# Causal attention in a hybrid decoder layer: low keys zero-padded to 128 rows, value products in one 65-column group, division left to the head norm

## Chip, cores and metric

The kernel runs on one core of one Trainium2 chip. The metric is the device time of one execution in microseconds (us), the median of several runs.

## The reference, cut to what matters

One layer of a decoder trunk over 2048 tokens of width 1024. Eight attention heads of width 64 with a forget gate, and four mLSTM heads of width 128, share one input projection; their outputs are normed per head and go through `W_out`, then an MLP (1024 to 4096 to 1024) and a gated embedding follow. The part that the change touches:

```python
def fox_attention(q, k, v, f_pre):            # q, k, v: (1, 2048, 8, 64)
    c = cumsum(log_sigmoid(f_pre))            # per head
    for each block i of 128 queries:
        s = q_i @ k.T * 64 ** -0.5 + c_query - c_key
        s = where(key <= query, s, -inf)
        o_i = softmax(s) @ v
    return o

def head_rmsnorm(h, g):                       # per token and head, over 64 values
    return h * rsqrt(mean(h * h) + 1e-6) * g
```

## The kernel before

**Precision by halves.** Every operand of a matmul is float16, split into a high and a low part, so a product is a sum of three: high by high, high by low, low by high. A projection (`z_feature`, `z_token`) is 24 accumulating matmuls: 8 blocks of 128 inputs by 3.

**Stages.** In order of time: RMSNorm and transposition of x; mLSTM head by head, to about 530 us; attention in four pairs of heads, 558 to 1347 us; `W_out`, MLP and gated embeddings, from 1347 us on.

**One pair of heads.** `fox_attn` goes through both heads of a pair, and for each through nine groups of query blocks (`ROWS`: block 15, the pairs 14 and 0 to 8 and 6, block 7), so that a group has 16 key blocks, and the last has 8. For each group:

- `fox_rows` makes scores in pieces of up to 512 keys. Line 782 multiplies 128 rows of queries (64 high, 64 low) by 128 rows of keys (the high keys twice). Line 784 adds high queries by low keys, on 64 rows: rows 0 to 63 for the first head of a pair, 64 to 127 for the second, out of one tile `KL` that both heads share. Line 787 adds the mask where the piece reaches the diagonal. VectorE adds the gate bias, stores the sum and keeps the row maximum (line 790). ScalarE takes the exponential (805), then ScalarE makes the high half of the weights (810, tile `ph`, four buffers) and GpSimd, one time in eight VectorE, the low half (812). A transposing DMA on SP's queue brings both halves into `pt` (814, three buffers).
- `fill` emits pieces of other work in step with the length of the rows, from `pair_parts`: the next pair's projections (`fox_z`) and a share of `p @ W_ple` (`ple_parts`, which uses the second half of `KL`'s allocation as scratch). For the last pair the pieces are the mLSTM half of `W_out`. Projections and these pieces share four PSUM buffers, `psz`.
- `fox_av`, three groups later (`LAG`), multiplies the transposed weights by the values. A row of the value tile `vt` is a one, 64 high values, 64 low values: 129 columns. Per key block two matmuls accumulate in `av`, one PSUM bank with one buffer: high weights by all 129 columns (827), low weights by the first 65 (828). Column 0 is then the sum of weights. For each query block VectorE takes its reciprocal (834), ScalarE scales the columns of low values (836), and VectorE scales the high ones and adds (837), into `og`.
- `fox_post`, some groups later again, takes 512 tokens of a pair: squares on GpSimd (918), their sum, the inverse root by Newton steps on VectorE, the scaling, high and low halves, a transposing DMA and a store to `mixd` (a transposing DMA into `mix` for the last pair). It has a tile `po` of its own, whose halves are used in turn (`po_half`).

**Low halves of the projections.** `fox_z` has ScalarE write the high half of queries, values and keys, and VectorE the low half right behind it (lines 731, 733, 748, 755).

**Order.** Within an engine the instructions stand in the order that a planner gives them from its own estimates of durations and of free buffers; it follows the order of the program closely, but may put a score matmul among the value products of another group. Each engine then works through its list strictly in that order, and waits on semaphores.

Of the kernel before, what the change touches and what calls it, by code (L numbers as in the profile page):

```python
# [36 lines left out]
AB = 1  # L37
# [18 lines left out]
def hybrid_layer(ctx, tc, x, p, w_in, b_fox_f, b_mlstm_i, b_mlstm_f, w_conv, g_mix,  # L56
# [42 lines left out]
    def rstd_of(v, w, name, c=1.0):  # L99
        """c / sqrt(v) for v [P, w]: a first guess from the exponent and three Newton steps."""  # L100
# [59 lines left out]
    def prep_rows(w, r0, name, pool):  # L160
        """W rows r0..r0+256 (all 1024 columns) as hi and lo fp16 with one power of two."""
# [22 lines left out]
    def norm_T(pool, yp, g, xs, nm, ss=None):  # L184
        """rmsnorm (gain left out) of the 4 token tiles xs as transposed hi/lo tiles."""
# [98 lines left out]
    class Carve:  # L284
        """small tiles cut from larger ones"""
# [17 lines left out]
    def gates(gp, gpp):  # L303
# [16 lines left out]
        # columns of gz: 8 fox f, 4 mlstm i, 4 mlstm f  # L320
# [11 lines left out]
        # log_sigmoid(x) = min(x, 0) - log1p(exp(-|x|))  # L332
# [31 lines left out]
        # global cumulative sums of the fox gates, as rows  # L364
# [17 lines left out]
        # mlstm stabiliser  # L382
# [98 lines left out]
    with phase("mq", 1) as mq, phase("mbig", 1) as mb, phase("mc", 2) as mc, \  # L481
# [6 lines left out]
        for h in range(MH):  # L488
# [43 lines left out]
            # head rmsnorm of num / max(|den|, exp(-m)), times the output gate  # L532
# [42 lines left out]
    def ple_parts(sp, t0, t1):  # L575
        """p @ W_ple for token tiles t0 to t1, emitted one at a time between query rows"""
# [48 lines left out]
    # ---- W_out: weights, and the share of the mLSTM features, kept in DRAM -  # L625
# [5 lines left out]
    def wo_prep(r, b):  # L631
        """rows of half r (0: FoX, 1: mLSTM) and columns of half b"""
# [40 lines left out]
    vts, cur, fk, fhl, fst = {}, {}, {}, {}, {}  # L673

    def second_keys():
        """keys of the second head of a pair, once the pair before is through"""
# [7 lines left out]
    def pair_parts(j, box):  # L684
        """while pair j is at work: projections of the next one, a share of p @ W_ple"""
        z = fox_z(j + 1, box)
        pl = ple_parts(fk[1][:, 1], *((0, 5), (5, 10), (10, 16))[j])
# [7 lines left out]
    def fox_z(j, box):  # L695
        """projections of head pair j, emitted piece by piece; box gets what attention needs"""
# [25 lines left out]
        K, KL = fk[0], fk[1][:, 0]  # L722
        QA, QB, KA, KB = Q[:, 0], Q[:, 1], K[:, 0], K[:, 1]
        vtile(j)
        for g in range(G):
# [5 lines left out]
            V.scalar_tensor_tensor(QA[64:128, gs], ps[0:64], QS, QA[0:64, gs],  # L731
                                   ALU.mult, ALU.subtract)
            V.scalar_tensor_tensor(QB[0:64, gs], ps[64:128], QS, QB[64:128, gs],
                                   ALU.mult, ALU.subtract)
# [8 lines left out]
        for t in range(NT):  # L743
# [4 lines left out]
            V.scalar_tensor_tensor(vt[:, t, :, 65:129], src, QS, vt[:, t, :, 1:65],  # L748
                                   ALU.mult, ALU.subtract)
        for g in range(G):  # L750
# [4 lines left out]
            V.scalar_tensor_tensor(KL[0:64, gs], ps[0:64], QS, KA[0:64, gs],  # L755
                                   ALU.mult, ALU.subtract)
            V.tensor_copy(KA[64:128, gs], KA[0:64, gs])
            second.append((KB, KL, ps, gs))
        box.append((fs, iv, vt, ((QA, KA, KL, 0), (QB, KB, KL, 64))))
# [5 lines left out]
    def fox_rows(fl, fpp, h, rows, bias, fs, qkl):  # L765
        """scores and softmax weights of the query blocks rows of head h, side by side in
        units of 8 key blocks; returns the transposed weights of each unit"""
        Qt, Kt, KL, r0 = qkl
# [5 lines left out]
        for r, i in enumerate(rows):  # L774
            qs = slice(i * P, (i + 1) * P)
            mx, kb, parts = None, 0, []
            while kb <= i:
# [6 lines left out]
                PE.matmul(ps[:, 0:n * P], lhsT=Qt[r0:r0 + 64, qs], rhs=KL[r0:r0 + 64, ks],  # L784
                          start=False, stop=not diag)
# [32 lines left out]
    def fox_av(fl, fpp, h, rows, pts, vt, ogs):  # L818
        """weighted values of the query blocks, over the sums of the weights"""
        aps = fpp.tile([P, 512], F32, tag="av", name=f"av{h}_{rows[0]}", bufs=AB)  # L820
        at = 0
        for r, i in enumerate(rows):
            ar = aps[:, 256 * r:256 * r + 129]
            for kb in range(i + 1):
                pt, o = pts[(at + kb) // 8], (at + kb) % 8
                vs = vt[:, kb, (h % 2), :]
                PE.matmul(ar, lhsT=pt[:, o, :], rhs=vs, start=kb == 0, stop=False)  # L827
                PE.matmul(ar[:, 0:65], lhsT=pt[:, 8 + o, :], rhs=vs[:, 0:65],
                          start=False, stop=kb == i)
            at += i + 1  # L830
        for r, i in enumerate(rows):
            ar = aps[:, 256 * r:256 * r + 129]
            rs = fl.tile([P, 1], F32, tag="rs", name=f"rs{h}_{i}", bufs=8)
            V.reciprocal(rs, ar[:, 0:1])
            t1 = fl.tile([P, FD], F32, tag="t1", name=f"t1{h}_{i}", bufs=2)
# [4 lines left out]
    posts, avq, loads = [], [], []  # L840
# [9 lines left out]
    def mix_load(lo, hi):  # L850
        """finished mixed features back into SBUF, a piece at a time"""
# [16 lines left out]
    def fox_attn(fl, fpp, j, z, fill):  # L868
        fs, iv, vt, qkls = z
        ogs = {}  # L870
        cur[1] = 0
        cur[0] = fl.tile([P, S], F16, tag="po", name=f"po{j}", bufs=1)
        for hh in range(2):
# [9 lines left out]
            for k, rows in enumerate(ROWS):  # L883
                pts = fox_rows(fl, fpp, h, rows, bias, fs, qkls[hh])
                for i in rows:
                    if hh == 0 and i // 4 not in ogs:
                        ogs[i // 4] = fl.tile([P, 4, 2, FD], F32, tag="og",
# [22 lines left out]
    def po_half():  # L910
        cur[1] ^= 1
        return cur[0][:, cur[1] * 1024:cur[1] * 1024 + 1024]

    def fox_post(fl, j, g, og_, iv):
        """head rmsnorm of 512 tokens of a head pair, transposed into the mixed features."""
        og = og_.rearrange("p q h d -> p (q h) d")
        sq = po_half().bitcast(F32).rearrange("p (q d) -> p q d", d=FD)
# [3 lines left out]
        V.tensor_scalar(ss, ss, iv[:, 1:2], EPS, op0=ALU.mult, op1=ALU.add)  # L921
# [223 lines left out]
```

## Time and profile before

| | |
|---|---|
| time, three runs | 2997.50, 3002.49, 3008.02 us; median 3002.49 |
| span of the profiled execution | 2998.0 us, so the median lies 4.5 us above it |
| TensorE busy over the span | 2747.0 us (92%) |
| VectorE busy | 1676.0 us (56%) |
| ScalarE busy | 1049.3 us (35%) |
| GpSimd busy | 751.9 us (25%) |
| attention, from first score to last value product | about 558 to 1347 us |

In the profile PE is TensorE, PEld its weight loads, DVE VectorE, ACT ScalarE, POOL GpSimd, and SPq the queue that issues DMAs for SyncE. L784 is line 784 of the kernel before. A matmul's duration contains its way through the array, and the next one starts before it ends: what a matmul costs in a stream is the distance from its start to the next start, the pitch. A wait is written "who <- for whom".

### The profile page before, as it was taken

What the parts mean: (1) busy time and instruction counts of PE and PEld (TensorE: products, weight loads), DVE (VectorE), ACT (ScalarE), POOL (GpSimd) and SP (SyncE); (2) the same over time, 40 slices, a digit from 0 to 9 for tenths busy, and PEclk for the clock granted to TensorE, in tenths of its full rate; (3) what the DMA queues carried; (4) which work ended last, traced back from release to release, by engine and by line L of the source; (5) the groups of instructions that cost most, each with busy time, mean ns of one, the idle gap of its engine ahead of it and who ended that gap; (6) DMA issues with size and microseconds to landing.
All of it is one profiled execution on the core that took longest, in us unless ns stands there. A gap on an engine that the chain in (4) does not pass through costs nothing. (4 is left out here: it accounts for less than half of the span.)

```text
span 2998.0 us, 43441 instructions
## 1 busy us (share of the span) xinstructions
PE 2747.0 (92%) x17141; PEld 1483.3 (49%) x17141; DVE 1676.0 (56%) x3764; ACT 1049.3 (35%) x1878; POOL 751.9 (25%) x529
## 2 busy tenths in 40 slices
PE   4998999889888787888899999999999999999996
PEld 2766767454453443443344444444444444444785
DVE  6464654666858667557754454444544544445526
ACT  6244444465655564553411111111111111114432
POOL 1001100233433343243122111111121111111454
PEclk9999999999999998999999999999999999999998
DMA  9112220486876797896700000000000000003513
GB/s 246 38 44 57 57 50 22 112 156 131 146 148 132 150 200 187 190 201 218 149 29 29 29 29 29 15 26 17 29 29 28 29 29 29 28 15 70 112 43 141
DMA packets 539869, 256.27 MB, mean 85 GB/s; under 512 B 433296, under 2 KB 511376, under 8 KB 539664
## 3 DMA queue, kind: packets, MB, share of 16 engines
q1 hardware_dynamic: 529904, 236.67, 34.8%
q10 hardware_dynamic: 9760, 16.82, 1.7%
q8 instruction: 134, 2.20, 0.3%
q14 instruction: 71, 0.58, 0.1%
HBM read 113.88 MB, written 32.60 MB: 49 GB/s over the span
## 5 line engine op out<-in xcount | busy, mean ns | idle before, releaser
L1029 PE MATMUL d<-wd_hl,hid 128*128 128x512 f16 x3072 | 677.2, 380 | 10.7 <-DVE x L1034 10.6
L1011 PE MATMUL h<-y1t,wu_hl 128*128 128x512 f16 x3072 | 673.5, 379 | 2.5 <-ACT y1y L201 2.5
L1029 PEld LDWEIGHTS <-hid 128*128 128x128 f16 x3072 | 301.1, 98 | 376.6 <-issue 16.8
L1011 PEld LDWEIGHTS <-wu_hl 128*128 128x128 f16 x3072 | 300.5, 98 | 365.2 <-ACT y1y L201 3.0
L1034 DVE SCALAR_TENSOR_TENSOR x<-d,fac,x 128x512 f32<-128x512 f32 x512 | 373.5, 747 | 132.2 <-PE d L1029 132.1
L1019 POOL TENSOR_TENSOR hid<-r,hid 128x512 f16<-128x512 f32 x128 | 174.7, 1365 | 772.3 <-ACT hid L1018 666.4
L1017 DVE SCALAR_TENSOR_TENSOR r<-h,r 128x512 f32<-128x512 f32 x128 | 88.3, 690 | 461.6 <-ACT r L1015 461.5
L1015 ACT ACTIVATE r<-h 128x512 f32<-128x512 f32 x128 | 76.0, 594 | 768.9 <-PE h L1011 768.9
L812 POOL TENSOR_TENSOR ph<-sp,ph 128x1024 f16<-128x1024 f32 x119 | 255.8, 2162 | 311.5 <-ACT ph L810 216.3
L272 PEld LDWEIGHTS <-yt 128*128 128x128 f16 x3072 | 245.0, 100 | 37.0 <-issue 15.0
L261 PE MATMUL zqk<-yt,wqk_hl 128*128 128x512 f16 x768 | 188.0, 392 | 27.0 <-DMA yt<-yy 27.0
L805 ACT ACTIVATE sp<-sp,nb,fs 128x1024 f32<-128x1024 f32 (+3 forms) x192 | 179.1, 982 | 50.4 <-DVE nb L802 34.9
L991 PE MATMUL pg<-wpg_hl,y2t 128*128 128x256 f16 x1536 | 173.3, 276 | 17.6 <-ACT emb L1110 13.6
L272 PE MATMUL zvo<-wvo_hl,yt 128*128 128x256 f16 x1536 | 174.7, 275 | 4.8 <-ACT wvo_hl L156 3.5
L782 PE MATMUL s<-K,Q 128*128 128x512 f16 (+3 forms) x320 | 117.5, 367 | 62.7 <-DVE mx L790 61.1
L991 PEld LDWEIGHTS <-y2t 128*128 128x128 f16 x1536 | 151.9, 99 | 39.1 <-issue 19.7
L810 ACT CAST ph<-sp 128x1024 f16<-128x1024 f32 x136 | 139.0, 1038 | 71.5 <-DMA pt<-ph 71.3
L827 PE MATMUL av<-vt,pt 128*128 128x129 f16 x1088 | 115.5, 229 | 49.2 <-DVE og L837 29.3
L790 DVE CUSTOM_DVE_ANT_0 sp<-s,bias,mx 128x512 f32<-128x512 f32 (+2 forms) x192 | 124.0, 646 | 17.8 <-POOL ph L812 5.1
L827 PEld LDWEIGHTS <-pt 128*128 128x128 f16 x1088 | 102.8, 102 | 53.1 <-issue 31.9
L261 PEld LDWEIGHTS <-wqk_hl 128*128 128x128 f16 x768 | 77.4, 101 | 104.0 <-ACT wqk_hl L156 24.9
L642 PEld LDWEIGHTS <-mix 128*128 128x128 f16 x768 | 74.1, 101 | 99.9 <-issue 26.8
(378 smaller groups left out, 3581.3 us busy)
## 6 DMA issues: line engine op xcount, KB each, us to landing
x<-in_x_dram SPq DMA_DIRECT2D x32, 512.0 KB, 4.6
wu_st<-in_w_up_dram SPq DMA_DIRECT2D x16, 1024.0 KB
wd_st<-in_w_down_dram SPq DMA_DIRECT2D x16, 1024.0 KB, 4.9
bias<-crow SPq DMA_DIRECT2D x16, 512.0 KB, 5.1
pled<-fox_st ACTq DMA_DIRECT2D x32, 256.0 KB, 3.0
wod<-spare ACTq DMA_DIRECT2D x32, 256.0 KB, 3.5
wos<-wod SPq DMA_DIRECT2D x32, 256.0 KB, 3.5
emb<-pled SPq DMA_DIRECT2D x64, 128.0 KB, 2.1
```

The costliest lines, as they stand in the source:

```text
L261: PE.matmul(ps, lhsT=hl[:, a, kt, m * P:(m + 1) * P], rhs=yT[g][b][:, kt, :], start=i == 0, stop=i == 3 * KT - 1)
L272: PE.matmul(ps[:, 0:n], lhsT=yT[g][b][:, kt, o:o + P], rhs=hl[:, a, kt, 0:n], start=i == 0, stop=i == 3 * KT - 1)
L790: V.tensor_tensor_reduce(out=st[u][:, o * P:(o + n) * P], in0=ps[:, 0:n * P], in1=bias[kb // 8][:, kb % 8 * P:(kb % 8 + n) * P], scale=1.0 ...
L805: A.activation(sl_, sl_, AF.Exp, bias=nb, scale=fs[:, 0:1])
L810: A.copy(ph[:, 0:1024], st[u])
L812: eng.tensor_sub(ph[:, 1024:2048], st[u], ph[:, 0:1024])
L827: PE.matmul(ar, lhsT=pt[:, o, :], rhs=vs, start=kb == 0, stop=False)
L991: PE.matmul(ps, lhsT=aT[t // 4][ya][:, kt, o:o + P], rhs=hl[:, wa, kt, :], start=i == 0, stop=i == 3 * KT - 1)
L1011: PE.matmul(ps, lhsT=wu[:, a, kt, m * P:(m + 1) * P], rhs=y1T[g][b][:, kt, :], start=i == 0, stop=i == 3 * KT - 1)
L1019: T.tensor_sub(hid[:, 1, m], r2, hid[:, 0, m])
L1029: PE.matmul(ps, lhsT=hid[:, a, m, t * P:(t + 1) * P], rhs=wd[:, b, m, hf * 512:(hf + 1) * 512], start=i == 0, stop=i == 5)
L1034: V.scalar_tensor_tensor(xs, ps, fac, xs, ALU.mult, ALU.add)
```

## The change

Four edits; comment lines, which were removed as well, are left out here.

1. The low keys of the two heads of a pair get a half tile each, `KLA` and `KLB`, whose other 64 rows are set to zero once. The matmul of line 784 then takes all 128 rows of queries and of low keys.
2. A value product is three matmuls per key block into one group of 65 columns: high weights by one and high values, high weights by low values into the same columns 1 to 64, low weights by one and high values. The 65 sums are copied as they are into `og`; the division by the sum of weights is left out, and `fox_post` norms the undivided values with epsilon times the squared sum in place of epsilon. `av` becomes one tile of one bank, with two places used in turn.
3. The low halves of queries, values and keys in `fox_z` are put off (the diff shows the values'): each is emitted two pieces later, and all that are open are emitted when `fill` or `second_keys` begins.
4. `fox_post` takes its two work tiles from the ring `ph` of the softmax weights; the tile `po` is gone. `ple_parts` gets scratch of its own.

```diff
+    def defer(fn):
+        lows.append(fn)
+        if len(lows) > 2:
+            lows.pop(0)()
+    def flush():
+        while lows:
+            lows.pop(0)()
     def second_keys():
+        flush()
...
+            T.memset(fk[1][64:128, 0], 0.0)
+            T.memset(fk[1][0:64, 1], 0.0)
-        K, KL = fk[0], fk[1][:, 0]
+        K, KLA, KLB = fk[0], fk[1][:, 0], fk[1][:, 1]
...
-            V.scalar_tensor_tensor(vt[:, t, :, 65:129], src, QS, vt[:, t, :, 1:65],
-                                   ALU.mult, ALU.subtract)
+            defer(lambda t=t, src=src: V.scalar_tensor_tensor(
+                vt[:, t, :, 65:129], src, QS, vt[:, t, :, 1:65], ALU.mult, ALU.subtract))
...
-                PE.matmul(ps[:, 0:n * P], lhsT=Qt[r0:r0 + 64, qs], rhs=KL[r0:r0 + 64, ks],
-                          start=False, stop=not diag)
+                PE.matmul(ps[:, 0:n * P], lhsT=Qt[:, qs], rhs=KL[:, ks], start=False,
+                          stop=not diag)
...
-        aps = fpp.tile([P, 512], F32, tag="av", name=f"av{h}_{rows[0]}", bufs=AB)
+        if not avt:
+            avt.append(fpp.tile([P, 2, 2, P], F32, name="av", bufs=1))
+        slot[0] ^= 1
+        aps = avt[0][:, slot[0]]
...
-                PE.matmul(ar, lhsT=pt[:, o, :], rhs=vs, start=kb == 0, stop=False)
-                PE.matmul(ar[:, 0:65], lhsT=pt[:, 8 + o, :], rhs=vs[:, 0:65],
-                          start=False, stop=kb == i)
+                PE.matmul(ar, lhsT=pt[:, o, :], rhs=vs[:, 0:65], start=kb == 0, stop=False)
+                PE.matmul(ar[:, 1:65], lhsT=pt[:, o, :], rhs=vs[:, 65:129], start=False,
+                          stop=False, skip_group_check=True)
+                PE.matmul(ar, lhsT=pt[:, 8 + o, :], rhs=vs[:, 0:65], start=False, stop=kb == i)
...
-            V.reciprocal(rs, ar[:, 0:1])
-            A.activation(t1, ar[:, 65:129], AF.Copy, scale=rs)
-            V.scalar_tensor_tensor(ogs[i // 4][:, i % 4, h % 2, :], ar[:, 1:65], rs, t1,
-                                   ALU.mult, ALU.add)
+            V.tensor_copy(ogs[i // 4][:, i % 4, h % 2, :], aps[:, r, 0:65])
...
-        sq = po_half().bitcast(F32).rearrange("p (q d) -> p q d", d=FD)
+        of = og_.rearrange("p q h d -> p (q h) d")
+        lw, og = of[:, :, 0], of[:, :, 1:FD + 1]
+        sq = fl.tile([P, 2048], F16, tag="ph", name=f"psq{j}_{g}", bufs=PHB)
...
-        V.tensor_scalar(ss, ss, iv[:, 1:2], EPS, op0=ALU.mult, op1=ALU.add)
+        V.scalar_tensor_tensor(el, lw, EPS, lw, ALU.mult, ALU.mult)
+        V.scalar_tensor_tensor(ss, ss, iv[:, 1:2], el, ALU.mult, ALU.add)
...
+        po = fl.tile([P, 2048], F16, tag="ph", name=f"po{j}_{g}", bufs=PHB)
...
             def fill(n):
+                flush()
...
+                    plsp[0] = fl.tile([P, S], F16, name="plsp", bufs=1)
```

## Rows read from the trace of the kernel before

**Rows 1.** The page: busy time of each engine, share of the span, instructions.
```profile
PE 2747.0 (92%) x17141; PEld 1483.3 (49%) x17141; DVE 1676.0 (56%) x3764; ACT 1049.3 (35%) x1878; POOL 751.9 (25%) x529
```
**Rows 2.** Stretches by pair: length, PE, PEld, DVE, ACT, POOL busy; granted clock; DMA share; GB/s.
```profile
558.00:744.00 186.00, 162.29 (x1294) 85.61 (x1293) 123.95 (x393) 111.69 (x163) 73.69 (x38) 0.94 0.68 130
744.00:933.00 189.00, 160.00 (x1366) 89.61 (x1364) 141.12 (x440) 111.21 (x168) 73.58 (x40) 0.94 0.77 147
933.00:1120.00 187.00, 156.55 (x1367) 86.01 (x1365) 132.02 (x404) 104.74 (x160) 74.39 (x39) 0.94 0.81 163
1120.00:1347.00 227.00, 180.22 (x1232) 85.64 (x1233) 145.34 (x417) 120.28 (x169) 86.72 (x45) 0.89 0.86 192
```
**Rows 3.** Waits from 558 to 1347 us: total us, times, longest.
```profile
ACT ph L810 <- DMA pt<-ph: 71.3, 39, 6.8
PE s L782 <- DVE mx L790: 61.1, 35, 8.1
...
DVE KL L755 <- ACT K L754: 30.8, 8, 5.2
PE av L827 <- DVE og L837: 29.3, 13, 8.9
...
PE av L827 <- DMA pt<-ph: 12.9, 11, 2.5
```
**Rows 4.** Timeline of PE from 1027.4 us: start, duration, line.
```profile
1027.47 0.38 PE L782 MATMUL s<-K,Q 128*128 128x512 f16 x1
1027.78 0.39 PE L784 MATMUL s<-KL,Q 64*128 64x512 f16 x1
...
1028.42 0.39 PE L784 MATMUL s<-KL,Q 64*128 64x512 f16 x1
1028.74 0.23 PE L787 MATMUL s<-fneg,identb 128*128 128x128 bf16 x1
1028.80 0.38 PE L782 MATMUL s<-K,Q 128*128 128x512 f16 x1
```
**Rows 5.** Timeline of the weight loads, same place, with the idle time before.
```profile
1027.77 0.09 PEld L784 LDWEIGHTS <-Q 64*128 64x128 f16 x1 [0.24 <-issue]
```
**Rows 6.** The chain of waits, in the MLP: start, length, 48 matmuls of 512 columns.
```profile
2212.16 10.36 PE h L1011 x48
```
**Rows 7.** Line 784 alone: number and durations in ns.
```profile
L784 PE MATMUL s<-KL,Q x320: 226/386/606, 559.1 to 1311.8; 64*128 64x512 f16 x120, 64*128 64x256 f16 x24, 64*128 64x128 f16 x8, 64*128 64x384 f16 x8
```
**Rows 8.** Timeline of PE: 16 key blocks of value products, then a score.
```profile
1007.57 0.22 PE L827 MATMUL av<-vt,pt 128*128 128x129 f16 x1 [1.16 <-DVE pm L584]
...
1007.65 0.22 PE L827 MATMUL av<-vt,pt 128*128 128x129 f16 x1
...
1008.96 0.22 PE L782 MATMUL s<-K,Q 128*128 128x128 f16 x1
```
**Rows 9.** Groups by shape: busy us and mean ns of one.
```profile
L317 PE MATMUL gz<-wg_hl,yt 128*128 128x16 f16 x384 | 10.1, 172 | 0.0
L827 PEld LDWEIGHTS <-pt 128*128 128x128 f16 x1088 | 102.8, 102 | 53.1 <-issue 31.9 <-DMA pt<-ph 15.5 <-DMA KL<-in_p_dram 1.4
```
**Rows 10.** The tile `av`: durations in ns, least, median, most.
```profile
L834 DVE RECIPROCAL rs<-av x128: 148/159/170, 596.6 to 1345.0; 128x1 f32<-128x1 f32 x128
L836 ACT ACTIVATE t<-av,rs x128: 293/314/316, 596.9 to 1345.3; 128x64 f32<-128x64 f32 x128
L837 DVE SCALAR_TENSOR_TENSOR og<-av,rs,t x128: 262/278/285, 600.5 to 1345.6; 128x64 f32<-128x64 f32 x128
```
**Rows 11.** A copy of 129 columns out of PSUM, in the mLSTM stage.
```profile
L514 DVE COPY num<-n x4: 293/294/295, 180.7 to 475.5; 128x129 f32<-128x129 f32 x4
```
**Rows 12.** A stretch of 100 us, columns as in Rows 2.
```profile
900.00:1000.00 100.00, 85.31 (x626) 41.39 (x625) 85.48 (x229) 56.67 (x81) 37.67 (x21) 0.91 0.69 131
```
**Rows 13.** The tile `po` in one `fox_post`, 720 to 760 us.
```profile
L927 ACT CAST po<-og x1: 618/618/618, 739.2 to 739.2; 128x512 f16<-128x512 f32 x1
...
L932 SPq DMA_DIRECT2D mixd<-po x1: 671/671/671, 749.9 to 749.9; - x1
```

More of the change, by code (lines that the diff above doesn't have):

```diff
@@ L36 @@
 SB = 3
-AB = 1
 RC = 2.0
@@ L672, in hybrid_layer @@
     second = []
-    vts, cur, fk, fhl, fst = {}, {}, {}, {}, {}
+    vts, plsp, fk, fhl, fst = {}, {}, {}, {}, {}
+    lows = []
+    def defer(fn):
[5 more added lines that the diff above has]
+            lows.pop(0)()
     def second_keys():
+        flush()
         for KB, KL, ps, gs in second:
@@ L686, in pair_parts @@
         z = fox_z(j + 1, box)
-        pl = ple_parts(fk[1][:, 1], *((0, 5), (5, 10), (10, 16))[j])
+        pl = ple_parts(plsp[0], *((0, 5), (5, 10), (10, 16))[j])
         for i, n in enumerate(z):
@@ L730, in fox_z @@
             A.activation(QB[64:128, gs], ps[64:128], AF.Copy, scale=QS)
-            V.scalar_tensor_tensor(QA[64:128, gs], ps[0:64], QS, QA[0:64, gs],
-                                   ALU.mult, ALU.subtract)
-            V.scalar_tensor_tensor(QB[0:64, gs], ps[64:128], QS, QB[64:128, gs],
-                                   ALU.mult, ALU.subtract)
+            defer(lambda ps=ps, gs=gs: (
+                V.scalar_tensor_tensor(QA[64:128, gs], ps[0:64], QS, QA[0:64, gs],
+                                       ALU.mult, ALU.subtract),
+                V.scalar_tensor_tensor(QB[0:64, gs], ps[64:128], QS, QB[64:128, gs],
+                                       ALU.mult, ALU.subtract)))
         hk, pwk = prep(FK, 0, "wfk")
@@ L754, in fox_z @@
             A.activation(KA[0:64, gs], ps[0:64], AF.Copy, scale=QS)
[L755 to L759, printed above, removed]
+            defer(lambda ps=ps, gs=gs: (
+                V.scalar_tensor_tensor(KLA[0:64, gs], ps[0:64], QS, KA[0:64, gs],
+                                       ALU.mult, ALU.subtract),
+                V.tensor_copy(KA[64:128, gs], KA[0:64, gs])))
+            second.append((KB, KLB, ps, gs))
+        box.append((fs, iv, vt, ((QA, KA, KLA), (QB, KB, KLB))))
     cnt = [0]
@@ L765, in fox_rows @@
     def fox_rows(fl, fpp, h, rows, bias, fs, qkl):
-        Qt, Kt, KL, r0 = qkl
+        Qt, Kt, KL = qkl
         tag = f"{h}_{rows[0]}"
@@ L826, in fox_av @@
                 vs = vt[:, kb, (h % 2), :]
-                PE.matmul(ar, lhsT=pt[:, o, :], rhs=vs, start=kb == 0, stop=False)
-                PE.matmul(ar[:, 0:65], lhsT=pt[:, 8 + o, :], rhs=vs[:, 0:65],
-                          start=False, stop=kb == i)
+                PE.matmul(ar, lhsT=pt[:, o, :], rhs=vs[:, 0:65], start=kb == 0, stop=False)
+                PE.matmul(ar[:, 1:65], lhsT=pt[:, o, :], rhs=vs[:, 65:129], start=False,
+                          stop=False, skip_group_check=True)
+                PE.matmul(ar, lhsT=pt[:, 8 + o, :], rhs=vs[:, 0:65], start=False, stop=kb == i)
             at += i + 1
         for r, i in enumerate(rows):
-            ar = aps[:, 256 * r:256 * r + 129]
-            rs = fl.tile([P, 1], F32, tag="rs", name=f"rs{h}_{i}", bufs=8)
-            V.reciprocal(rs, ar[:, 0:1])
-            t1 = fl.tile([P, FD], F32, tag="t1", name=f"t1{h}_{i}", bufs=2)
-            A.activation(t1, ar[:, 65:129], AF.Copy, scale=rs)
-            V.scalar_tensor_tensor(ogs[i // 4][:, i % 4, h % 2, :], ar[:, 1:65], rs, t1,
-                                   ALU.mult, ALU.add)
-    posts, avq, loads = [], [], []
+            V.tensor_copy(ogs[i // 4][:, i % 4, h % 2, :], aps[:, r, 0:65])
+    posts, avq, loads, avt, slot = [], [], [], [], [0]
     def drain(n):
@@ L870, in fox_attn @@
         ogs = {}
-        cur[1] = 0
-        cur[0] = fl.tile([P, S], F16, tag="po", name=f"po{j}", bufs=1)
         for hh in range(2):
@@ L886, in fox_attn @@
                     if hh == 0 and i // 4 not in ogs:
-                        ogs[i // 4] = fl.tile([P, 4, 2, FD], F32, tag="og",
+                        ogs[i // 4] = fl.tile([P, 4, 2, FD + 1], F32, tag="og",
                                               name=f"og{j}_{i // 4}", bufs=4)
@@ L920, in fox_post @@
         V.tensor_reduce(ss, sq, axis=AX.X, op=ALU.add)
-        V.tensor_scalar(ss, ss, iv[:, 1:2], EPS, op0=ALU.mult, op1=ALU.add)
+        el = fl.tile([P, 8], F32, tag="el", name=f"fel{j}_{g}", bufs=2)
+        V.scalar_tensor_tensor(el, lw, EPS, lw, ALU.mult, ALU.mult)
+        V.scalar_tensor_tensor(ss, ss, iv[:, 1:2], el, ALU.mult, ALU.add)
         rr = rstd_of(ss, 8, f"frr{j}_{g}", YS)
@@ L924, in fox_post @@
         V.tensor_mul(og, og, rr.unsqueeze(2).to_broadcast([P, 8, FD]))
-        mh = po_half().rearrange("p (a s) -> p a s", a=2)
-        of = og_.rearrange("p q h d -> p (q h d)")
-        A.copy(mh[:, 0], of)
-        V.tensor_sub(mh[:, 1], of, mh[:, 0])
+        po = fl.tile([P, 2048], F16, tag="ph", name=f"po{j}_{g}", bufs=PHB)
+        mh = po[:, 0:1024].rearrange("p (a s) -> p a s", a=2)
+        mq = mh.rearrange("p a (q d) -> p a q d", d=FD)
+        A.copy(mq[:, 0], og)
+        V.tensor_sub(mq[:, 1], og, mq[:, 0])
         if j < NP - 1:
-            mT = po_half().rearrange("p (t s) -> p t s", s=P)
+            mT = po[:, 1024:2048].rearrange("p (t s) -> p t s", s=P)
             SP.dma_start_transpose(out=mT, in_=mh.rearrange("p a s -> p (a s)"))
```

8 lines of the change are left out of this document (2 added, 6 removed).

## The prediction

> **What bounds the kernel now.** I read the page first, for the share of each engine: TensorE is busy 92% of the span [rows 1], so a change counts where it shortens TensorE's list or its waits. Everything that the diff touches lies between 558 and 1347 us, so the second view is the table of stretches, one for each pair of heads [rows 2]. The reader is to see three things there. TensorE is busy for 659 of the 789 us (the four rows added), so it idles 130 us, a sixth, where the MLP is nearly full. VectorE is next with 542 us, and no engine is full. The DMA share grows from 0.68 to 0.86 over the pairs. The third view is the list of waits of that stretch [rows 3]: TensorE waits 61.1 us for row maxima (a score's PSUM buffer comes free only when VectorE has read it) and 29.3 us for the eviction of value products, but only 12.9 us for the transposing DMAs. From 1347 us on, `W_out` runs without a wait on attention, so time saved before that point is time saved at the end. What sets the end is TensorE's list plus its waits for VectorE; the fourth view, the timeline, shows what that list is made of.
>
> **Low keys on 128 rows.** In the timeline [rows 4] line 784 starts 0.31 us after line 782 and line 787 starts 0.32 us after line 784, all with 512 columns in front. A stream of 512-column matmuls whose weights all have 128 rows goes at 10.36/48 = 0.216 us [rows 6], each with a weight load of its own. So a step from 128 to 64 rows costs 0.10 us, and the step back as much. Line 787 to line 782, both on 128 rows, takes 0.06 us for 128 columns, with nothing on top. The weight loads say why: the one of line 784 starts after 0.24 us of idleness, 0.01 us before its matmul [rows 4, 5]; it doesn't run ahead of the matmul in flight. There are 320 such matmuls [rows 7], each with a step in front and one behind: 640 x 0.10 = 64 us of TensorE's list. With 128 rows the columns stay the same, and no step is left. The bounds: 64 us if all is the step, 0 if the extra comes from something that stays. I take 64, since the step from 787 to 782 has none of it. The zeros are two fills on GpSimd, once, about 474 us, beside the last mLSTM head; GpSimd idles 75% of the span [rows 1]. Bare, each would cost about 2.5 us, an estimate from ScalarE's 0.618 us for 512 columns [rows 13] times four.
>
> **Three value products for two.** A pair of line 827 and line 828 with 129 + 65 = 194 columns has a pitch of 0.08 to 0.09 us; 16 of them take 1.39 us, 0.087 each [rows 8]. That is 194 columns at 2.4 GHz (0.081 us, granted clock 0.94 in these stretches, [rows 2]) and 3 ns for each matmul. The change has 65 + 64 + 65, again 194, and one matmul more. If that costs only its 3 ns, 1088 of them cost 3 us. From above: its weight load fully bare, 0.102 us each, makes 111 us [rows 9]. I take 3 us, because 384 matmuls of 16 columns, each with 128x128 weights, took 10.1 us, 0.026 us each [rows 9]: a load in a stream hides down to that, and 64 columns take 0.027 us.
>
> The Trainium skill, "TensorE: Matmul & The Clock Gate", section "LDWEIGHTS (loading the stationary operand)", gives columns / 1.2 in ns, an estimate of 107 ns for each such load; if the third load were bare by that rule, it would cost 1088 x 0.107 = 116 us. The trace does not agree that loads are bare, at 0.026 us for load and matmul together [rows 9].
>
> **Eviction.** Each of 128 query blocks now takes 0.159 us of VectorE, 0.314 of ScalarE and 0.278 of VectorE in a row [rows 10]. It becomes one copy of 65 columns, which the trace doesn't have; it lies between a one-column operation (0.159) and a 129-column copy (0.294, [rows 11]), and I take 0.22. For a group of two blocks the chain falls from 2 x 0.751 = 1.50 us on two engines to 0.44 on one, by 70%. TensorE's 29.3 us wait for that chain [rows 3], so 21 us go; the bounds are 0 and 29. Off the path, VectorE gets 128 x (0.437 - 0.22) = 28 us back, less about 4 us for one more small operation in each of 16 `fox_post` calls, and ScalarE 40.
>
> The two places of the new `av` do not overlap a copy with the next group's products in this sum: both lie in one bank, and the wait in the trace is on the bank's only buffer. The Trainium skill, "PSUM — Partial Sum Buffer", section "PSUM bank collisions raise a hardware error", says that TensorE must not write a bank while VectorE reads it, at whatever address, and that the guard goes by bank. By that rule the wait stays and gets shorter, as above; without it all 29 us would go. No row here shows two places in a bank.
>
> **Put-off low halves.** VectorE now stands still behind ScalarE's high half, 30.8 us for keys alone [rows 3]; behind it stand row maxima, for which TensorE waits. Two pieces later the high half is long done, so that stall goes. What is late next is the PSUM buffer: two of four in `psz` stay taken until the next `fill`, behind that group's row maxima, and TensorE's next piece may wait for one. Bounds: a third of the 61.1 us wait gained, 20; lost, about 40 (half of the 54 groups with projections by 1.5 us, an estimate a little under the 61.1/35 = 1.7 us of a mean wait for row maxima, [rows 3]). I take 0, between them.
>
> **Row maxima.** The 61.1 us pull both ways: VectorE has some 24 us less to do, but TensorE comes to it sooner. Bounds: half of the wait gained, 30, or 24 lost (second rival). I take 0.
>
> **Post tiles in the ring.** Each of 16 `fox_post` takes two of the four `ph` buffers. One, `po`, is held from 739.2 to beyond 749.9 us in the call shown [rows 13], and ScalarE, next in the ring, already waits 71.3 us, 1.8 on average and 6.8 at most [rows 3]. Behind ScalarE's cast stand exponentials and the evictions of projections; behind those TensorE. Bounds: 0, since ScalarE is busy only 448 of 789 us [rows 2], and 16 x 6.8 = 109. I take 16 x 2 x 1.8 = 58 us of ScalarE waits, and pass on the share that reaches TensorE now, 12.9 of 71.3 [rows 3]: 10 us. The scratch for `ple_parts` moves nothing: its loads, transposes and issues are the same, and so is their place on SP's queue. `fox_post` issues the same DMAs from another tile.
>
> **Sum.** -64 + 3 - 21 + 10 = -72 us against the profiled execution's 2998.0, so 2926. The median of the runs lies 4.5 us above that span: 2931 us.
>
> **Rivals.** 0.3% (9 us) is about what separates a change from none here.
>
> *VectorE becomes the bound.* In three stretches of 100 us out of eight VectorE is as busy as TensorE (one of them, 85.48 against 85.31, [rows 12]). If TensorE's saving there turns into waits for row maxima, 3/8 x 64 = 24 us come back, and the 21 of the eviction with them: -72 + 45 = -27, 2976 us. For it speaks that row; against it, that VectorE loses 24 us of work and the stalls behind ScalarE.
>
> *More goes than counted.* All of the eviction wait, half of that for row maxima, nothing lost in the ring: -64 + 3 - 29 - 30 = -120, 2882 us. The 130 idle us in [rows 2] leave room.
>
> *The ring makes it slower.* If every post stalls ScalarE for the longest wait seen, and all of it reaches TensorE, the term is 109 for 10: -72 + 99 = +27, 3030 us. It turns the sign once more than 82/16 = 5.1 us of each post reaches TensorE. For it speaks the time that `po` is held; against it, that of 71.3 us waited for `ph` only 12.9 show as TensorE's wait for `pt`.
>
> *The third weight load is bare.* -72 + 111 - 3 = +36, 3039 us. The rule cited above would do this; the 16-column stream speaks against it [rows 9].
>
> *The padding does nothing*, because the 0.10 us has another cause: +3 - 21 + 10 = -8, 2995 us. Against it speaks line 787 before line 782 [rows 4].
>
> **Chances.** Forecast 0.40; VectorE 0.25; more 0.15; ring 0.08; bare load 0.03; no effect of padding 0.06; 0.03 for orders of the planner that none of these is, split evenly over the signs. Faster: 0.40 + 0.25 + 0.15 + 0.01 = 0.81, rounded up to 0.82; same 0.07; slower 0.11. The forecast's own range is 2905 to 2955; the first three cases, 0.80 together, reach from 2870 to 2985, with the unknown bounds of put-off halves and ring around 2882 and 2976.
>
> **What would show it.** Padding: line 784's pitch 0.22 us, its weight load ahead of time, TensorE's busy time in 558 to 1347 us near 600. Value products: three matmuls in 0.09 us per key block; 0.15 or more would mean a bare load. Eviction: TensorE's wait for `av` near 8 us. Ring: ScalarE's waits for `ph` under 130 us; with well over that, and TensorE waiting for `pt` or for projections' evictions, the forecast is wrong. VectorE: a wait for row maxima beyond 85 us would prove the second rival.

## The result, and the profile after

| | before | after |
|---|---|---|
| median | 3001.89 us | 2980.52 us (2976.74 to 2985.34, 4 runs) |
| ratio | | 0.9923, 95% interval 0.9900 to 0.9945 |
| span of the profiled execution | 2998.0 us | 2979.7 us |
| last value product starts at | 1344.8 us | 1321.7 us |
| from there to the end of the span | 1653.2 us | 1658.0 us |

One execution of the kernel "ring and padding" below, 3949 us at a granted clock of 0.66, is left out; all the others are fast ones.

The change makes the kernel faster, by 21 us of the 72 forecast. The page after gives the busy time of each engine, to be set beside [rows 1]:

```profile
PE 2698.7 (91%) x18229; PEld 1505.7 (51%) x18229; DVE 1617.3 (54%) x3652; ACT 1016.6 (34%) x1750; POOL 761.6 (26%) x531
```

TensorE has 48 us less to do, VectorE 59 and ScalarE 33, and yet the span falls by 18. The four pairs of heads after, in the columns of [rows 2]:

```profile
560.00:740.00 180.00, 147.99 (x1594) 91.70 (x1592) 119.69 (x351) 105.15 (x137) 75.97 (x38) 0.94 0.70 136
740.00:919.00 179.00, 139.60 (x1532) 89.58 (x1531) 116.92 (x395) 99.04 (x132) 71.27 (x37) 0.93 0.74 145
919.00:1098.00 179.00, 142.91 (x1574) 91.99 (x1574) 117.48 (x375) 96.24 (x127) 71.11 (x37) 0.93 0.81 162
1098.00:1322.00 224.00, 174.39 (x1632) 94.86 (x1632) 131.95 (x400) 115.02 (x135) 95.12 (x48) 0.91 0.92 202
```

TensorE's 659 busy us have become 605, near the 600 forecast. The stretch, however, shrank only from 789 to 762 us, so its idle time grew from 130 to 157 us. Where it went is in the list of waits after, from 558 to 1325 us, beside [rows 3]:

```profile
PE s L798 <- DVE mx L806: 84.2, 47, 6.3
ACT sp L821 <- DVE nb L818: 71.8, 24, 11.2
...
ACT ph L826 <- DMA pt<-ph: 60.0, 26, 5.8
PE av L846 <- DMA pt<-ph: 53.2, 36, 5.9
...
DVE sp L806 <- POOL ph L828: 31.1, 19, 5.4
...
DVE KL L771 <- ACT K L769: 20.0, 6, 3.9
...
PE av L846 <- DVE og L852: 9.1, 6, 3.1
```

TensorE's wait for the eviction fell from 29.3 to 9.1 us, as forecast. Its wait for row maxima rose from 61.1 to 84.2 us and its wait for the transposing DMAs from 12.9 to 53.2 us. These two take 63 us more, where TensorE's list and its wait for the eviction had given back 74. The rest of the idle time, many small waits, fell from 27 to 11 us, so that 27 us of stretch are left as gain.

The padding did on TensorE what was forecast. The timeline of PE after shows it, where the list has scores only, beside [rows 4]:

```profile
1041.52 0.38 PE L798 MATMUL s<-K,Q 128*128 128x512 f16 x1
1041.74 0.38 PE L800 MATMUL s<-KL,Q 128*128 128x512 f16 x1
1041.95 0.38 PE L798 MATMUL s<-K,Q 128*128 128x512 f16 x1
1042.17 0.38 PE L800 MATMUL s<-KL,Q 128*128 128x512 f16 x1
```

The timeline of its weight loads, beside [rows 5]:

```profile
1041.52 0.10 PEld L800 LDWEIGHTS <-Q 128*128 128x128 f16 x1
```

The pitch is 0.21 to 0.22 us where it was 0.31 and 0.32, and the load of line 800 starts 0.22 us before its matmul, under the matmul ahead. The Trainium skill, "TensorEngine Tiling (Array Packing)", section "Key Properties", says that changing the tiling mode drains TensorE; the trace agrees so far as 0.10 us at each change of height is gone when all weights have 128 rows. The drain itself is in no row.

The value products after, beside [rows 8], and the copy that replaces the three operations of [rows 10]:

```profile
955.53 0.19 PE L846 MATMUL av<-vt,pt 128*128 128x65 f16 x1
955.56 0.20 PE L847 MATMUL av<-vt,pt 128*128 128x64 f16 x1
955.60 0.19 PE L849 MATMUL av<-vt,pt 128*128 128x65 f16 x1
955.63 0.19 PE L846 MATMUL av<-vt,pt 128*128 128x65 f16 x1
...
L852 DVE COPY og<-av x128: 206/218/228, 594.1 to 1322.8; 128x65 f32<-128x65 f32 x128
```

Three products take 0.10 us in the first of these and 0.09 in the next ones, so the third weight load is hidden; the copy takes 0.218 us where 0.22 was estimated. These prices were right, then, and the sum was not.

### The profile page after: what moved, and what is told of

Its sections match the earlier page's. It is cut to its first block, busy times and chain, and to the rows that moved or that the text cites. A ratio compares the mean times of both kernels' runs of the same rounds, so it can differ in the third digit from the quotient of the medians.

```text
span 2979.7 us, 45372 instructions
## 1 busy us (share of the span) xinstructions
PE 2698.7 (91%) x18229; PEld 1505.7 (51%) x18229; DVE 1617.3 (54%) x3652; ACT 1016.6 (34%) x1750; POOL 761.6 (26%) x531
## 5 line engine op out<-in xcount | busy, mean ns | idle before, releaser
L798 PE MATMUL s<-K,Q 128*128 128x512 f16 (+3 forms) x320 | 119.3, 373 | 86.8 <-DVE mx L806 84.2
L846 PE MATMUL av<-vt,pt 128*128 128x65 f16 x1088 | 120.3, 198 | 62.4 <-DMA pt<-ph 53.2
```

What stands on the lines that cost most here:

```text
L846: PE.matmul(ar, lhsT=pt[:, o, :], rhs=vs[:, 0:65], start=kb == 0, stop=False)
```

## Experiments

Two theories. **A, a bound:** TensorE's list and its waits for VectorE set the end, as the prediction had it, and some part of the change other than the padding costs what is missing. **B, a chain:** no engine sets the pace through attention; each engine has a fixed list and waits for others in turn, so that the 64 us of the padding count only where a low-key matmul lies on the chain of waits. In the recorded expectations A is the TensorE theory. B stands there as the loop theory, at first in a narrower form: the round of buffers from a score to their release sets the pace. A third one, the ring theory, has the post tiles in the ring eat the padding's gain. Each kernel was timed beside the kernel before. A difference "of before" is (ratio - 1) x 3002 us.

### The parts one by one, on the kernel before

**Ring alone**: post tiles from `ph`, nothing else.

```diff
-        sq = po_half().bitcast(F32)...
+        sq = fl.tile([P, 2048], F16, tag="ph", name=f"psq{j}_{g}", bufs=PHB)
...
-        mh = po_half()...
+        po = fl.tile([P, 2048], F16, tag="ph", name=f"po{j}_{g}", bufs=PHB)
```

> The kernel before with one part alone: the post tiles in the ring of the softmax weights, no tile of their own. Ring theory (the two ring places per post are what ate the padding's gain): 30 to 50 us slower than before, 3030 to 3050. Loop theory (the round from a score to the release of its buffers sets the pace, the ring's extra tenants matter little): within 10 us of before.

**Ring and padding**: the low-key tiles `KLA` and `KLB`, their two fills and the scratch on top.

```diff
+            T.memset(fk[1][64:128, 0], 0.0)
+            T.memset(fk[1][0:64, 1], 0.0)
...
-  lhsT=Qt[r0:r0 + 64, qs], rhs=KL[r0:r0 + 64, ks]
+  lhsT=Qt[:, qs], rhs=KL[:, ks]
```

> The kernel before with the padded low keys and, for the room that they need, the post tiles in the ring; nothing else changed. Prediction's own working: 64 us less TensorE and 10 lost in the ring, 54 us faster, 2948. Loop theory: TensorE's busy time falls by 60 but its waits grow by 35 or more, 10 to 25 us faster, 2977 to 2992. Ring theory: the same 10 to 25, but then the ring alone is 30 to 50 slower.

**Division**: three products, undivided copy, division in the head norm.

```diff
-                PE.matmul(ar, lhsT=pt[:, o, :], rhs=vs, start=kb == 0, stop=False)
+                PE.matmul(ar, lhsT=pt[:, o, :], rhs=vs[:, 0:65], start=kb == 0, stop=False)
+                PE.matmul(ar[:, 1:65], lhsT=pt[:, o, :], rhs=vs[:, 65:129], ...)
...
+            V.tensor_copy(ogs[i // 4][:, i % 4, h % 2, :], aps[:, r, 0:65])
```

> The kernel before with three value products per key block, undivided sums copied out, and the division in the head norm; nothing else changed. Prediction's working: -21 of the eviction wait and +3, so 18 us faster, 2984. Loop theory: VectorE and ScalarE are links of the round and get 28 and 40 us of work less, so 5 to 20 us faster. A cost of the third product would make it slower by up to 100.

**Put-off low halves** of queries, keys and values.

```diff
-            V.scalar_tensor_tensor(QA[64:128, gs], ps[0:64], QS, ...)
+            defer(lambda ps=ps, gs=gs: (V.scalar_tensor_tensor(QA[64:128, gs], ...
```

> The kernel before with the low halves of the projections put off by two pieces; nothing else changed. Prediction's working: 0, bounds -20 and +40. Theory that the put-off halves hold the PSUM buffers of the projections: 15 to 40 us slower, and TensorE waits for the projections' buffers. Loop theory: within 10 us, with the stalls of VectorE behind ScalarE gone and other waits in their place.

| kernel | median us | ratio to before (95%) | of before | forecast term |
|---|---|---|---|---|
| ring | 2984.38 | 0.9940 (0.9918 to 0.9962) | -18 | +10 |
| ring and padding | 2976.72 | 0.9915 (0.9882 to 0.9948) | -25.5 (padding: -7.5) | padding -64 |
| division | 3009.46 | 1.0027 (1.0011 to 1.0044) | +8 | +3 - 21 = -18 |
| put-off low halves | 2994.90 | 0.9974 (0.9962 to 0.9986) | -8 | 0 |
| the whole change | 2980.52 | 0.9923 (0.9900 to 0.9945) | -23 | -72 |

The ring theory falls: the ring alone was to be 30 to 50 us slower and is 18 faster, which is also more than the 10 us that the loop theory allowed. Division was forecast faster by both theories, and is slower. Ring and padding came out where the loop theory put them (2977 to 2992, at its edge), put-off halves within its 10 us. The stall that this part was to remove is still there, however; with the put-off halves alone, beside the 30.8 us of [rows 3]:

```profile
DVE KL L769 <- ACT K L767: 29.3, 7, 5.4
```

The parts add to -25.5, the whole to -23, so the shortfall is not in their meeting. Most of it is in the padding, 56 us, at about an eighth of its term; division falls short by 26, and ring and put-off halves give 36 more than forecast. Attention in the two kernels that differ by it, columns as in [rows 2]; first the ring alone:

```profile
558.00:1318.00 760.00, 655.04 (x5248) 345.36 (x5248) 499.45 (x1633) 449.64 (x660) 310.02 (x159) 0.93 0.80 164
```

Then the ring and the padding:

```profile
564.00:1322.00 758.00, 598.85 (x5250) 361.65 (x5249) 496.74 (x1627) 448.59 (x661) 312.65 (x159) 0.93 0.80 166
```

At the same granted clock, 0.93, TensorE's work falls by 56 us and the stretch by 2. Their waits, of the ring alone:

```profile
PE s L782 <- DVE mx L790: 52.4, 36, 4.6
...
PE av L827 <- DVE og L837: 17.0, 12, 3.9
PE av L827 <- DMA pt<-ph: 16.4, 11, 3.2
```

Of the ring and the padding:

```profile
PE s L785 <- DVE mx L793: 89.5, 58, 5.7
...
PE av L830 <- DVE og L840: 24.6, 14, 4.9
PE av L830 <- DMA pt<-ph: 19.9, 13, 3.7
```

Of the 56 us saved, 37 come back as waits for row maxima, 8 at the eviction and 4 at the transposes. VectorE had no more to do (499 and 497 us busy): TensorE comes to it sooner and waits.

### The whole change without the padding

```diff
+        r0 = 64 * (h % 2)
...
-  lhsT=Qt[:, qs], rhs=KL[:, ks], start=False,
+  lhsT=Qt[r0:r0 + 64, qs], rhs=KL[r0:r0 + 64, ks], start=False,
```

> The changed kernel without the padding alone: 64-row low keys in one shared tile, scratch of the embedding share back in its second half; value products, division, put-off halves and ring stay. Prediction's working: 61 us slower than the changed kernel, 3040. Loop theory, after 5 us between the two kernels with the ring alone and ring with padding: 0 to 15 us slower, 2980 to 2995.

Median 2999.16 us, ratio 0.9974 (0.9954 to 0.9994). So the padding, added to the other three edits, brings 15 us. Attention without it:

```profile
560.00:1349.00 789.00, 682.09 (x6323) 360.91 (x6322) 486.59 (x1522) 415.18 (x529) 310.66 (x159) 0.89 0.78 158
```

TensorE has 77 us more than after, at a granted clock of 0.89 in place of 0.93; part of the 15 us may be that clock, which the pair above doesn't have. Its wait for row maxima, to be set beside the 84.2 us after:

```profile
PE s L797 <- DVE mx L805: 53.6, 33, 6.4
```

So here too the padding made this wait longer, by 31 us. Both forecasts missed: 3040 by far, 2980 to 2995 by 4 us. Ring, division and put-off halves alone would add to -18, and -8 was measured; without the padding the parts do not simply add.

### TensorE's work cut further

The matmul of line 800 is taken out of the kernel after; the low keys are left out of the scores, about 62 us of TensorE's list.

```diff
-                PE.matmul(ps[:, 0:n * P], lhsT=Qt[:, qs], rhs=KL[:, ks], start=False,
-                          stop=not diag)
```

> The changed kernel without the matmul of queries by low keys (left out altogether): 320 matmuls or 60 to 65 us less on TensorE, nothing else touched. TensorE theory (its list sets the end): 50 us or more faster than the changed kernel, 2930 or less. Loop theory (the round of buffers through the other engines sets the pace): within 12 us of the changed kernel's 2980, TensorE's waits up by about what was cut.

Median 2953.92 us, ratio 0.9831 (0.9816 to 0.9845): 27 us under after, less than half of what was cut. Waits of this kernel:

```profile
PE av L845 <- DMA pt<-ph: 88.0, 62, 6.4
...
PE s L799 <- DVE mx L805: 67.1, 52, 12.4
```

Attention in it, columns as in [rows 2]:

```profile
558.00:1300.00 742.00, 561.95 (x6011) 342.14 (x6010) 484.69 (x1516) 414.24 (x530) 311.27 (x159) 0.90 0.83 169
```

Now most of TensorE's wait is for the transposes, 88.0 us against 53.2. The granted clock fell to 0.90, so TensorE is busy for only 43 us less than after, in a stretch that is 20 us shorter. A bound by TensorE's list, which A needs, would have passed on nearly all. The result lies between the two forecasts (2930 or less, and within 12 us of 2980): TensorE's work counts, by about half.

### Transposing DMAs halved, with and without padding

Only the high half of the weights is transposed, and the third value product takes high weights again: the low weights are left out of the result.

```diff
-            SP.dma_start_transpose(out=pt, in_=ph)
+            SP.dma_start_transpose(out=pt[:, 0:8], in_=ph[:, 0:1024])
...
-  lhsT=pt[:, 8 + o, :], rhs=vs[:, 0:65]
+  lhsT=pt[:, o, :], rhs=vs[:, 0:65]
```

With padding:

> The changed kernel with the transposing DMA of the softmax weights cut to its high half, the products with low weights reading the high ones: half of the DMA bytes of the weights left out, all else the same. DMA theory (transposes at their rate or their way to landing set the pace): 30 us or more faster than 2980. Loop through ScalarE, GpSimd and VectorE: less than 15 us.

Without (on the whole change without the padding):

> The changed kernel without the padding and with the transposing DMA of the weights cut to the high half, products with low weights reading the high ones (low weights left out of the DMA). Against s_halfT (2947), which has the padding. Theory that the transposes take up what the padding frees: padding worth 30 us or more here, 2977 or above. Theory that fixed lists spread any saving over many waits: worth 10 to 20 as before, 2957 to 2967.

With padding 2947.24 us, ratio 0.9813 (0.9796 to 0.9831); without, 2961.47 us, 0.9858 (0.9834 to 0.9883). Half of the transposes is worth 33 us with the padding and 35 without, and the padding 13.5 us here. So the forecasts of the DMA theory (30 us or more) and of fixed lists (2957 to 2967) came true. That the transposes swallow the padding's gain was a theory of mine; then the padding would have been worth more here than the 15 us above, so that theory falls. Halving them saves about as much with the padding as without.

This pair also settles the clock. Attention from 560 to 1290 us, first without the padding, then with it, where it ends 15 us sooner:

```profile
560.00:1290.00 730.00, 644.29 (x6227) 343.90 (x6227) 492.52 (x1502) 411.97 (x526) 309.87 (x158) 0.93 0.55 122
560.00:1290.00 730.00, 601.75 (x6355) 365.18 (x6356) 501.47 (x1543) 417.50 (x534) 311.70 (x160) 0.93 0.57 126
```

The granted clock is 0.93 in both, and the padding is worth 13.5 us; of the 15 us above little can be the clock. Their waits for row maxima, in the same order:

```profile
PE s L797 <- DVE mx L805: 64.7, 35, 7.0
PE s L798 <- DVE mx L806: 97.7, 52, 8.7
```

Once more 33 us come back as this wait, of 57 us that TensorE is busy for less over the span (2746.7 and 2689.7 us).

### More buffers

On the whole change without the padding, one ring deeper by one buffer at a time: does a buffer that comes free late set the pace?

```diff
-PTB = 3
+PTB = 4
```

> The kernel without padding, and the 4 KB that the padding needs for scratch given to a fourth buffer of transposed weights. Loop theory: the way from ph through the transposing DMA to pt is the longest part of the round, so 10 to 30 us faster than without it, 2955 to 2980. TensorE theory: within 8 us of n_base.

```diff
-PHB = 4
+PHB = 5
```

> The kernel without padding, the 4 KB given to a fifth buffer of the ring of softmax weights and post tiles. Loop theory: ScalarE's 50 to 70 us of waiting for this ring fall by half, 5 to 25 us faster than n_base. If ring places cost anything (prediction's term of 10 us), at least those 10. TensorE theory: within 8 us.

```diff
-SPB = 4
+SPB = 5
```

> The kernel without padding, the 4 KB given to a fifth buffer of the scores before the exponential. Loop theory: VectorE's wait for GpSimd to free these (7 us before, 31 after) goes, 5 to 20 us faster than n_base. TensorE theory: within 8 us.

Against 0.9974 without them: a fourth `pt` 2994.26 us, ratio 0.9966 (0.9952 to 0.9980); a fifth `ph` 3008.62 us, 1.0011 (0.9992 to 1.0030); a fifth `sp` 2999.68 us, 0.9982 (0.9964 to 1.0001). None gains what the padding missed, and the forecasts of the loop theory failed in all three: there is no sign here that a buffer that comes free late sets the pace. A fourth `pt` and a fifth `sp` stay within the 8 us of the TensorE theory, so on this kernel these runs don't speak against A. In the fifth `ph` one wait gave way to another. Two waits of the kernel without it:

```profile
ACT ph L825 <- DMA pt<-ph: 72.5, 30, 6.0
ACT sp L820 <- DVE nb L817: 70.3, 30, 11.7
```

With it, the first is not among the long waits any more, and the second took its place:

```profile
ACT sp L820 <- DVE nb L817: 129.0, 44, 10.1
```

ScalarE now stands still one step earlier, at the exponential, whose bias VectorE makes from the row maximum. The orders of these lists differ, too (next but one), and 9 us are within what that does.

### Work moved from GpSimd to VectorE

```diff
-DM = 8
+DM = 4
```

On the kernel after, VectorE makes one low half of the weights in four, where it was one in eight.

> The changed kernel with VectorE making the low half of the weights one time in four, not one in eight: 17 x 2.16 us less for GpSimd, 17 x 1.23 us more for VectorE. GpSimd as the slow link: 10 to 30 us faster than 2980. VectorE as the slow link: 10 to 25 us slower. Neither: within 8 us.

Median 2972.57 us, ratio 0.9896 (0.9877 to 0.9915), 8 us under after, with intervals that overlap, at the edge of the forecast "neither". More work for VectorE did not hurt, which speaks against VectorE as the bound; but the order of the lists changed as well, and 8 us are less than that alone can do (next section).

### Another order, the same work

`TOT` is a constant by which `fill` spaces its pieces; another value changes the order of the lists and no work.

```diff
-TOT = 60.0
+TOT = 52.0     (or 68.0)
```

> The kernel before with the pieces of other work emitted 13% later (weight total 52 for 60), no work changed. If order alone moves this kernel as it moved the changed one (+12 for 68): 8 to 20 us away from 3002 on either side. If not: within 6 us.

> The kernel before with the pieces of other work emitted 13% sooner (68 for 60), no work changed. As for b_tot52: 8 to 20 us away from 3002 if order alone does it, within 6 us if not.

> The changed kernel with the pieces of other work emitted 13% later (52 for 60). TensorE now has time to spare between scores, and pieces that come later fill it: 5 to 15 us faster than 2980. If the pace was right as it was: as much slower.

> The changed kernel with the pieces of other work emitted 13% sooner (weight total 68 for 60): no instruction more or less, only another order. Order theory (what an edit is worth here is mostly what the planner makes of it): 8 us or more in either direction. Otherwise within 5 us of 2980.

| `TOT` | before | after |
|---|---|---|
| 52 | 3007.92, ratio 1.0010 (0.9996 to 1.0024) | 2995.89, 0.9976 (0.9962 to 0.9990) |
| 60 | 3001.89 | 2980.52, 0.9923 (0.9900 to 0.9945) |
| 68 | 2990.89, 0.9958 (0.9944 to 0.9973) | 2992.47, 0.9962 (0.9945 to 0.9979) |

Order alone moves the time by up to 16 us. Two of the four forecasts saw it (68, before and after); 52 on the kernel before was within 6 us, and 52 after lost 15, as the second of its two forecasts had it. The whole change is worth 10, 23 and -1 us of before at the three values: the gain that was measured first is the best of three orders, and at 68 the kernels before and after are alike. So a single part of 8 or even 18 us may be its order and not its work. The granted clock over attention goes along only in part: before and after it is 0.90 and 0.91 at 52, 0.93 and 0.93 at 60, 0.91 and 0.93 at 68. The padding is free of that doubt: in all three pairs that differ by it (ring; whole change; halved transposes) the lists of the two kernels stand in the same order, all of TensorE's matmuls and 99% or more of every other engine's instructions. Cutting the low-key matmul, halving the transposes, one more buffer and `DM = 4` do change the order; of these only the 33 and 35 us for the transposes and the 27 us for the cut matmul are more than it was seen to do.

### The best of it

Padding, ring and put-off halves, with the value products and the eviction of before; and the same with `DM = 4`.

```diff
 (the edits of ring, padding and put-off halves; fox_av as before)
-DM = 8
+DM = 4     (second kernel only)
```

> The change without its value-product part: padding, ring and put-off halves, with the two products, the reciprocal and the eviction of before. If the parts' effects add up (-17, -5, -7): 29 us faster than before, 2973, and 8 faster than the whole change. If each is mostly the order that it brought: anywhere from 2970 to 3000.

> The same with VectorE making the low half of the weights one time in four. It gave 8 us on the whole change; here VectorE has 28 us more to do for evictions. If the 8 carry over: 2965. If VectorE has no room for them: no faster than c_nodiv.

The first takes 2971.64 us, ratio 0.9892 (0.9872 to 0.9912), -32 us of before where the parts add to -33.5. The second takes 2964.07 us, 0.9876 (0.9861 to 0.9890), and beats both kernels; it is clear of after (0.9900 to 0.9945), while the two of them are not clear of each other.

### The chain through attention

This is worked out from the traces, by the rule of the page's chain of waits: from the last value product back to the first score, at each step to what released it, or to the instruction before it on its engine. Once in each kernel, between 779 and 1128 us, the way back was lost, and was taken up again at TensorE's matmul of that time. Microseconds on the chain, by what they were spent in (DMA is from issue to landing; issuing on the queues, 23 to 42 us, is left out):

```
kernel             attention  TensorE   DMA  VectorE  GpSimd  ScalarE  issue   low-key matmuls
                                                                              on it, of 320
before                 786.2    257.7  169.6    210.1    29.6     44.7   51.8   139
ring                   760.4    244.6  164.6    118.8    73.3     47.7   83.0   136
ring and padding       757.8    123.7  185.7    150.7    88.2     78.1   89.5    69
without padding        788.9    285.1  184.1    112.1    60.6     44.3   71.7   143
after                  761.4    142.2  213.0    133.2    85.6     56.9  102.2    45
```

Before, TensorE is a third of the chain (258 of 786 us) although it is busy for five sixths of the time, and 139 of 320 low-key matmuls lie on it. At 2 x 0.10 us each, the padding had 28 us to take off this chain, not 64. With the padding, the chain goes another way: TensorE's part falls by 121 and 143 us in the two pairs, and the other parts grow by 118 and 115. So there must have been another chain, nearly as long, before: through transposing DMAs, GpSimd's low halves and VectorE's row maxima. That is B in its wide form. That a second chain was there is concluded from the first one's giving way; it was not traced in the kernel before. The 28 us are thus a ceiling for the padding; what it gave, 7.5 to 15 us, would be the distance to the next chain.

## Why the prediction was wrong

The sign was right; the size was not. The time lies inside the widest range (2870 to 2985), but outside the forecast's own (2905 to 2955). That even the wide one holds it is luck: its upper end came from the rival that VectorE becomes the bound, whose mechanism the runs don't show, and the misses of ring (28 us to the good) and division (26 to the bad) cancel.

- **The bound: the step that failed.** "What sets the end is TensorE's list plus its waits for VectorE", and from it "64 us if all is the step", taken in full. The price of a step was nearly right: 56 us of busy time gone in the ring pair, at equal clocks, where 64 were forecast. But it was 7.5, 13.5 and 15 us at the end, in three pairs of kernels. The first of these is not clear of zero by its intervals; the other two are. In all three pairs the wait for row maxima took 31 to 37 us of the saving. The fault was to read a busy share of 83% as the path that sets the end. I held waits of TensorE on others (61.1, 29.3 and 12.9 us, [rows 3]) to be what stands between list and span, and took them as fixed, or as falling. They depend on when TensorE comes: in the whole change the three grew by 43 us together, although the eviction's fell by 20.
- **Row maxima, taken as 0.** The bounds were half the wait gained or 24 us lost; measured, the wait rose by 23 us after, and by 37 us where the padding came alone. The prediction named a wait beyond 85 us as proof of the rival "VectorE becomes the bound". With 84.2 us the mark was nearly reached, with ring and padding it was passed (89.5), and the time of that rival (2976 us) is close to the one measured. Its mechanism isn't there, though: over attention VectorE is busy for 486 of 762 us after, where it was 542 of 789, and more work for it didn't slow the kernel. A wait for an engine doesn't show that the engine is full.
- **Third value product.** +3 us, and the price is as forecast: 0.09 to 0.10 us per key block. The rival of the bare load falls.
- **Eviction.** TensorE's wait for it fell by 20.2 us, where 21 was forecast. At the end nothing came of it: division alone made the kernel 8 us slower. In that kernel TensorE waits 23.7 us for the transposes (12.9 before), and the granted clock over attention is 0.90 (0.93 before). Whether this wait, the clock or the order is the cause of the +8 was not settled. That the wait became shorter and stayed, 9.1 us in 6 times, is what was forecast for two places in one bank.
- **Ring.** +10 forecast, -18 measured, so the rival that it makes the kernel slower falls. ScalarE's wait for `ph` fell from 71.3 to 54.2 us with the ring alone and to 60.0 in the whole change, where up to 130 was allowed for. Why the ring gains is open: the wait of `po` for its own DMA, which is gone, was only 3.6 us before, while the order changes, and order alone is worth up to 16 us.
- **Put-off halves.** 0 forecast, between -20 and +40; -8 measured, which is within what order does. "So that stall goes" did not come true. With the put-off halves alone the wait of VectorE behind ScalarE's high half is 29.3 us, where it was 30.8. The 20.0 us after are not the work of this part: with ring and padding, without it, the wait was 18.7 already.
- **From 1347 us on.** "Time saved before that point is time saved at the end": attention ends 23.1 us earlier and the rest takes 4.8 us longer, so 18.3 are left in the span. Small, and its cause was not looked for.

What stays open: the split of -18, +8 and -8 between mechanism, order and clock, and the second chain in the kernel before.

## What to carry to other kernels

A busy share, even the largest, doesn't say that an engine sets the pace: before pricing a saving at its full value, follow the chain of waits through the stage itself, and count how many of the shortened instructions lie on it (139 of 320 here). Where every engine works through a fixed list and waits on the others, cutting one engine's work is paid out at a fraction (here an eighth to a half), and the rest shows up as longer waits for whoever comes next. And measure what a mere change of order is worth (16 us here) before explaining a part that is smaller; compare kernels whose lists stand in the same order, where the edit allows it.

## What the runs showed of the hardware

- Going between weights of 64 and of 128 rows costs 0.10 us of TensorE each way, and 320 such matmuls in a stream of taller ones cost 56 us of busy time. On 128 rows, half of them zeros, it is gone.
- A 64-column matmul with a 128x128 weight load of its own takes 0.03 us in a stream: the third product per key block was nearly free.
- A copy of 65 columns out of PSUM takes 0.218 us on VectorE, and one of 129 takes 0.294 [rows 11].
- The granted clock over attention, a mean over stretches at the two levels, differed between kernels with almost the same work: 0.89 for the whole change without the padding, 0.90 with division alone, 0.93 before and after. It doesn't follow the padding: with halved transposes it is 0.93 without and with it.
